# The samples' new scan states: four plain fp32 products of 32 rows in four PSUM banks in place of eight fp32r products of split operands

## The chip, the core and the metric

The kernel runs on one core of one Trainium2 chip. The metric is the device time of one execution in microseconds. Five engines work side by side, each through its own list of instructions in order: TensorE (PE in the profile, with its weight loads as PEld), VectorE (DVE), ScalarE (ACT), GpSimd (POOL) and SyncE (SP). Here SP issues most of the DMAs, and POOL issues the stores of intermediate results besides some small arithmetic. PE writes its products into eight banks of PSUM; DVE and ACT read them from there. A product that is queued on PE waits until its operands are written and its bank has been read out.

## The reference

One inference step of a hybrid encoder layer for two groups of requests that share the weights: a prompt of 1024 tokens, and 8 sample batches of 16 tokens each. Each token goes through one wide input projection, then through band attention and through a Mamba-2 scan, whose results are merged and projected out. The change touches one line of the scan, the new state, and of it the part for the samples alone:

```python
def step(h, inp):
    x, d, bk, ck = inp
    a_cs = jnp.cumsum(d * ag, axis=1)
    ...
    xdt = x * d[..., None]
    ...
    to_end = jnp.exp(a_cs[:, -1:] - a_cs)
    h_new = h * jnp.exp(a_cs[:, -1])[..., None, None] + jnp.einsum('blgn,blgep->bgepn', bk, xdt * to_end[..., None])
    return h_new, y_in + y_st
```

For the samples a chunk is the 16 tokens of a batch, so the scan is one step. For each of the 8 batches and each pair of heads, the product of `bk` (16 tokens by 128 state entries) and the weighted `x` (16 tokens by 128 channels) is added to the decayed old state. There are 32 heads, handled as 16 pairs; four pairs form a group that shares `bk`.

## The kernel before, in words

The 1152 tokens (1024 prompt, then 128 sample tokens) lie along the columns. Every wide projection is made in fp16 with two-part operands: a weight block and a token block are each split into a high and a low part, and three products (high by high, high by low, low by high) are summed in PSUM. These are the products of `dense`, lines 872, 873 and 875, 128x384 each; `dense_tok` (lines 925 to 927) does the same for attention, and `quad_dense` (lines 781 to 783) for the last projections.

The stages are: attention of 8 head units with their projections; then 16 pairs of scan heads, each with its own projections; then the output projections. The pair's small work (`ssd`, lines 1864 to 2095) runs between the products of the projections. For a pair p, `main` does in order:

- It turns `x` to have tokens in the rows, and scales it in two ways: `xd`, and `xw`, which also carries the decay to the end of the chunk. `tokb` holds `bk` of the group with the tokens in the rows. Rows 0 to 127 of the last 128 columns are the 128 sample tokens, 16 rows a batch.
- Prompt states: products of line 1990, sums on DVE (line 1999), stored at line 2004.
- Outputs: products of lines 2018, 2025 and 2038 and their sums on DVE (lines 2031, 2043, 2044, 2051).
- The old sample states `h0` are scaled on DVE (line 2053); the outputs are stored at line 2055, issued by POOL.
- New sample states, lines 2059 to 2074: eight products of line 2063 (128x256, all 128 rows) and two additions to `h0` on DVE (line 2072), then the store of line 2081, issued by POOL.

A product that contracts over 128 rows would mix the batches, so the rows of the other batches have to be zero. Before the change this goes so. For each half of the batches (64 token rows) `bk` is split into a high part and a rest (`hi`, `lo`, lines 1962 to 1965, once a group), and `xw` likewise (lines 1971 and 1972, once a pair), in the type fp32r. The high part of `xw` sits in the half's own 64 rows and the rest in the other 64, so that a product over 128 rows sums both. `masked(q)` then copies this, on POOL, twice over into 256 columns, each copy with the rows of all batches but one zeroed (line 1979). There are two places for such masked operands, so `masked(2)` and `masked(3)` wait until the products of `masked(0)` and `masked(1)` have read theirs. Each masked operand is multiplied by `hi` and by `lo`.

PSUM has three pools: `d` with three banks for the projections, `g` with three banks for small work, and `s` with one place of two banks (`pss`), which the products of line 2018 and attention use.

The order of each engine's instructions is made ahead of the run by the class `Order`: it puts every instruction at a time by a table of costs, takes the earliest in program order that can go, keeps a margin for inputs that come from other engines (1000 ns for PE, 2500 ns for a DMA), and allots the PSUM places. Consecutive products of the same tile shape in parts of the array form one unit.

Of the kernel before, what the change touches and what calls it, by code (L numbers as in the profile page):

```python
# [49 lines left out]
C_ID, C_U, C_UB, C_ONE, C_BLK, C_BM, C_SEL, C_S4, C_BM4 = 0, 128, 256, 384, 512, 640, 648, 680, 712  # L50
NCONST = 716
# [369 lines left out]
def trunk_kernel(ctx: ExitStack, tc: tile.TileContext, h, again):  # L421
# [18 lines left out]
    def pg(cols=512):  # L440
        return psg.tile([P, 512], F32, tag="g", name=nm("g"))[:, :cols]
# [35 lines left out]
    bmask4 = cst[:, C_BM4:C_BM4 + 4]  # L477

# [39 lines left out]
    L_ST = rarena.set_layout(0, [("b", 4, P), ("s", 2, P), ("x", 2, 2 * P)])  # L518
# [1311 lines left out]
    def group_dense(g, lay):  # L1830
        res = grp[g] = {"b": [], "c": [], "sq": None, "st": None}
        yield from conv_gen(16 + g, lay, res["b"])
        yield from conv_gen(20 + g, lay, res["c"])
# [30 lines left out]
    def ssd(p):  # L1864
# [62 lines left out]
        def main():  # L1927
# [27 lines left out]
            if res["st"] is None:  # L1955
                bs = res["st"] = []
                for j in range(2):
                    rw, ro = slice(64 * j, 64 * j + 64), slice(64 - 64 * j, 128 - 64 * j)
                    b_ = tokb.ap[rw, NP:]
                    hi = yield from walloc(L_ST, "b", P)  # L1960
                    lo = yield from walloc(L_ST, "b", P)
                    nc.scalar.activation(hi.r[rw], b_, AF.Copy)
                    nc.scalar.activation(hi.r[ro], b_, AF.Copy)
                    nc.vector.tensor_tensor(lo.r[rw], b_, hi.ap[rw], ALU.subtract)
                    nc.vector.tensor_tensor(lo.r[ro], b_, hi.ap[rw], ALU.subtract)
                    bs.append((hi, lo))
            xs = []
            for j in range(2):
                rw, ro = slice(64 * j, 64 * j + 64), slice(64 - 64 * j, 128 - 64 * j)
                t = yield from walloc(L_ST, "s", P)  # L1970
                nc.scalar.activation(t.r[rw], xw.ap[rw, NP:], AF.Copy)
                nc.vector.tensor_tensor(t.r[ro], xw.ap[rw, NP:], t.ap[rw], ALU.subtract)
                xs.append(t)

            def masked(q):

                t = alloc(L_ST, "x", 2 * P)
                i = 2 * (q % 2)
                nc.gpsimd.tensor_tensor(t.r.rearrange("p (b n) -> p b n", n=P), xs[q // 2].ap.unsqueeze(1).to_broadcast([P, 2, P]),
                                        bmask4[:, i:i + 2].unsqueeze(2).to_broadcast([P, 2, P]), ALU.mult)  # L1980
                return t

            xm = [masked(0), masked(1)]
# [75 lines left out]
            pss_ = [pg(), pg()]  # L2059
            for q in range(4):  # L2060
                j, i = q // 2, q % 2
                for w, b_ in enumerate(res["st"][j]):
                    nc.tensor.matmul(pss_[j][:, 2 * i * P:2 * (i + 1) * P], b_.r, xm[q].r, start=w == 0, stop=w == 1)
                xm[q].free()
                if q < 2:
                    xm.append(masked(q + 2))
                yield 215
                if q == 1:
                    yield from pause(4500)
                if i:  # L2070
                    c = slice(4 * j * P, (4 * j + 4) * P)
                    nc.vector.tensor_tensor(h0.ap[:, c], h0.ap[:, c], pss_[j], ALU.add)
            for t in xs + [xw]:
                t.free()
# [8 lines left out]
            if p % PPG == PPG - 1:  # L2083
                s = res["sq"]
                for t in (tokb, res["cbm"], res["ct"], *res["st"][0], *res["st"][1]):
                    t.free()
# [2140 lines left out]
```

## Time and profile before

| what | value |
|---|---|
| median of 3 runs | 1749.53 us (1746.5 to 1753.16) |
| profiled execution: its time | 1750.06 us |
| profiled execution: its span | 1748.3 us |
| granted TensorE clock, mean | 0.995 |
| products of line 2063 | 128, from 703.0 to 1359.0 us |
| bytes moved by DMA | 284.92 MB |

The span is the time from the first to the last instruction of the profiled execution; 1.8 us lie around it. The columns of the profile's lists of groups are: line, engine, operation, what it writes and reads, shapes and count, then busy time in us, mean ns of one, idle time of the engine just before them and what ended it. A PE shape such as 128*32 is the part of the array that a product occupies, rows by columns. A product of plain fp32 stands in the trace as two records, one of fp16 or fp32r as one. The duration of a PE record contains its way through the array, so records overlap; what a product costs is read from the distance between starts.

### The profile page before, as it was taken

The page shows a single profiled execution, that of the slowest core. Times are in us where ns is not written, and L with a number is a line of the kernel's source. Part 1 is how long each engine was busy: PE and PEld are TensorE (multiplying, and loading weights), DVE is VectorE, ACT ScalarE, POOL GpSimd, SP SyncE. Part 2 cuts the span into 40 slices and gives each one's busy share as a digit, 9 for nine tenths or more (in the row PEclk, how much of TensorE's full clock was granted, in tenths as well). Part 3 has the DMA queues.
Part 4 walks back from the last instruction along what each step waited for, and adds up shares of the span by engine and source line. Part 5 has one row for each costly group of instructions (what it writes and reads, how often), then busy time and mean ns, then how long its engine had stood idle before and what let it go on. Part 6 is the DMA issues. An engine that isn't in the chain of part 4 may idle for free.

```text
span 1748.3 us, 35611 instructions
## 1 busy us (share of the span) xinstructions
PE 1718.8 (98%) x14013; PEld 1113.4 (64%) x14013; DVE 1312.6 (75%) x2477; ACT 995.8 (57%) x1987; POOL 351.4 (20%) x624
## 2 busy tenths in 40 slices
PE   7999999999999999999999999999999999999998
PEld 3556556556556566667666766676666677666676
DVE  6458667877776967787878777777778787897694
ACT  8766555566465665655755556555666633455340
POOL 0233233224134011232312122212112200000000
PEclk9999999999999999999999999999999999999999
DMA  9248888988878584643554355434555655421141
GB/s 383 76 126 204 191 218 204 200 221 196 203 226 173 148 214 133 171 131 118 170 160 116 118 133 175 140 117 108 155 165 194 244 192 222 146 89 54 58 157 72
DMA packets 267433, 284.92 MB, mean 163 GB/s; under 512 B 199724, under 2 KB 200376, under 8 KB 267256
## 3 DMA queue, kind: packets, MB, share of 16 engines
q1 hardware_dynamic: 258296, 253.90, 52.4%
q0 software_dynamic: 8960, 28.65, 4.4%
q8 instruction: 112, 1.84, 0.4%
q14 instruction: 65, 0.53, 0.1%
HBM read 192.70 MB, written 43.66 MB: 135 GB/s over the span
## 4 chain that ended last, share of the span: by engine, by line
PE 87%; ACT 4%; DVE 4%; DMA 2%; issue 1%; POOL 1%; SPq 0%; DVEq 0%; ACTq 0%; POOLq 0%
PE d L872 16%; PE d L873 16%; PE d L875 16%; PE d L925 5%; PE d L927 5%; PE d L926 5%; PE g L1531 2%; PE s L2018 2%; PE g L1990 2%; PE g L2038 1%; PE s L783 1%; PE s L781 1%; PE s L782 1%; PE s L1578 1%; PE g L1578 1%
## 5 line engine op out<-in xcount | busy, mean ns | idle before, releaser
L872 PE MATMUL d<-arena 128*128 128x384 f16 x1872 | 611.8, 327 | 1.4 <-ACT arena L1706 1.4
L873 PE MATMUL d<-arena 128*128 128x384 f16 x1872 | 610.7, 326 | 0.0
L875 PE MATMUL d<-arena 128*128 128x384 f16 x1872 | 610.7, 326 | 0.0
L875 PEld LDWEIGHTS <-arena 128*128 128x128 f16 x1896 | 185.7, 98 | 122.9 <-issue 0.5
L872 PEld LDWEIGHTS <-arena 128*128 128x128 f16 x1896 | 185.7, 98 | 121.5 <-issue 8.6
L873 PEld LDWEIGHTS <-arena 128*128 128x128 f16 x1896 | 185.7, 98 | 113.5 <-issue 2.0
L628 ACT ACTIVATE arena<-arena 128x1024 bf16<-128x1024 f32 (+4 forms) x185 | 184.6, 998 | 106.1 <-DMA arena<-in_wall_dram 65.4
L925 PE MATMUL d<-arena 128*128 128x384 f16 (+1 forms) x568 | 186.8, 329 | 0.0
L637 DVE SCALAR_TENSOR_TENSOR arena<-arena 128x1024 f16<-128x1024 f32 (+2 forms) x133 | 160.0, 1209 | 35.1 <-ACT arena L636 33.3
L927 PE MATMUL d<-arena 128*128 128x384 f16 (+1 forms) x568 | 186.1, 328 | 0.0
L926 PE MATMUL d<-arena 128*128 128x384 f16 (+1 forms) x568 | 186.1, 328 | 0.0
L636 ACT ACTIVATE arena<-arena 128x1024 f16<-128x1024 f32 (+2 forms) x133 | 135.5, 1021 | 85.3 <-PE d L873 15.5
L1471 ACT ACTIVATE arena<-arena 128x640 f32<-128x640 f32 (+4 forms) x144 | 100.8, 701 | 62.9 <-DVE arena L1474 62.4
L1729 DVE SCALAR_TENSOR_TENSOR arena<-arena 128x1176 f32<-128x1176 f32 x72 | 107.3, 1490 | 2.3 <-issue 0.9
L1917 ACT ACTIVATE arena<-arena 128x128 f32<-128x128 f32 x288 | 89.9, 390 | 25.9 <-DMA arena<-acs_d 25.7
L925 PEld LDWEIGHTS <-arena 128*128 128x128 f16 x576 | 56.3, 98 | 50.8 <-issue 17.5
L1507 DVE SCALAR_TENSOR_TENSOR arena<-arena 128x640 f16<-128x640 f32 (+4 forms) x128 | 87.0, 713 | 0.0
L1366 ACT ACTIVATE arena<-d 128x256 f32<-128x256 f32 x71 | 26.8, 377 | 96.1 <-PE d L927 96.0
L927 PEld LDWEIGHTS <-arena 128*128 128x128 f16 x576 | 56.4, 98 | 38.4 <-issue 0.2
L1399 POOL TENSOR_SCALAR arena<-arena 128x16 f32<-128x16 f32 (+1 forms) x24 | 9.4, 392 | 353.5 <-DVE arena L1372 353.4
L926 PEld LDWEIGHTS <-arena 128*128 128x128 f16 x576 | 56.4, 98 | 32.8
L1474 DVE CUSTOM_DVE_ANT_0 arena<-s,arena 128x320 f32<-128x320 f32 (+4 forms) x128 | 60.3, 503 | 19.4 <-PE s L1578 9.5
(271 smaller groups left out, 3150.0 us busy)
## 6 DMA issues: line engine op xcount, KB each, us to landing
arena<-in_wall_dram SPq DMA_DIRECT2D x85, 512.0 KB
arena<-acs_d SPq DMA_DIRECT2D x32, 576.0 KB
arena<-in_kc_dram SPq DMA_DIRECT2D x64, 256.0 KB
arena<-in_vc_dram SPq DMA_DIRECT2D x64, 256.0 KB
arena<-in_wada_dram SPq DMA_DIRECT2D x24, 512.0 KB
arena<-in_xT_dram SPq DMA_DIRECT2D x16, 576.0 KB
gate_d<-arena POOLq DMA_DIRECT2D x48, 192.0 KB, 3.6
arena<-eacs_d SPq DMA_DIRECT2D x32, 288.0 KB
```

The lines of the kernel that those rows point to most:

```text
L628: keep(nc.scalar.activation(junk[:, :n], x, AF.Square, scale=scale * n ** -0.5, accum_out=sums[:, c:c + 1]))
L636: keep(nc.scalar.activation(hi, x, AF.Copy, scale=scale))
L637: keep(nc.vector.scalar_tensor_tensor(lo, x, scale, hi, ALU.mult, ALU.subtract))
L872: nc.tensor.matmul(ps, hi.r[:, wc], kh.r[:, tok], start=k == 0, stop=False)
L873: nc.tensor.matmul(ps, hi.r[:, wc], kl.r[:, tok], start=False, stop=False)
L875: nc.tensor.matmul(ps, lo.r[:, wc], kh.r[:, tok], start=False, stop=k == nk - 1)
L925: nc.tensor.matmul(ps, kh.r[:, tok], wh, start=k == 0, stop=False)
L926: nc.tensor.matmul(ps, kh.r[:, tok], wl, start=False, stop=False)
L927: nc.tensor.matmul(ps, kl.r[:, tok], wh, start=False, stop=k == KT - 1)
L1471: nc.scalar.activation(p, p, AF.Exp, bias=sm_[:, 4 + e:5 + e], scale=-1.0, accum_out=sm_[:, 6 + e:7 + e])
L1729: nc.vector.scalar_tensor_tensor(yc, r.ap[:, j:j + n], w4[:, i, j:j + 1], yc, ALU.mult, ALU.add)
L1917: nc.scalar.activation(me[e].ap[:, cs], me[e].ap[:, cs], AF.Relu, scale=-1.0, bias=a4[:, c, hds[e]:hds[e] + 1])
```

## The change

The split parts go (the pools `b` and `s` of the fp32r store, and the instructions that made them). `xw` is masked once a pair, by POOL, with a new mask of two columns: column 0 is one where the batch of a row is even, column 1 where it is odd. A product over 32 rows (two batches) with this 256-column operand then gives the states of both batches side by side. Four such products, one for each 32 rows, in plain fp32, go to four banks: two of the pool `g` and both of the pool `s`. The pause of 4500 in the middle goes. DVE adds the four results in three additions: one for each `g` bank (256 columns), and one for both `s` banks.

```diff
-C_ID, C_U, C_UB, C_ONE, C_BLK, C_BM, C_SEL, C_S4, C_BM4 = 0, 128, 256, 384, 512, 640, 648, 680, 712
-NCONST = 716
+C_ID, C_U, C_UB, C_ONE, C_BLK, C_BM, C_SEL, C_S4, C_BM4, C_BM2 = 0, 128, 256, 384, 512, 640, 648, 680, 712, 716
+NCONST = 718
...
+    bmask2 = cst[:, C_BM2:C_BM2 + 2]
...
-    L_ST = rarena.set_layout(0, [("b", 4, P), ("s", 2, P), ("x", 2, 2 * P)])
+    L_ST = rarena.set_layout(0, [("x", 2, 2 * P)])
...
-            if res["st"] is None:
-                bs = res["st"] = []
-                for j in range(2):
-                    rw, ro = slice(64 * j, 64 * j + 64), slice(64 - 64 * j, 128 - 64 * j)
-                    b_ = tokb.ap[rw, NP:]
-                    hi = yield from walloc(L_ST, "b", P)
-                    lo = yield from walloc(L_ST, "b", P)
-                    nc.scalar.activation(hi.r[rw], b_, AF.Copy)
-                    nc.scalar.activation(hi.r[ro], b_, AF.Copy)
-                    nc.vector.tensor_tensor(lo.r[rw], b_, hi.ap[rw], ALU.subtract)
-                    nc.vector.tensor_tensor(lo.r[ro], b_, hi.ap[rw], ALU.subtract)
-                    bs.append((hi, lo))
-            xs = []
-            for j in range(2):
-                rw, ro = slice(64 * j, 64 * j + 64), slice(64 - 64 * j, 128 - 64 * j)
-                t = yield from walloc(L_ST, "s", P)
-                nc.scalar.activation(t.r[rw], xw.ap[rw, NP:], AF.Copy)
-                nc.vector.tensor_tensor(t.r[ro], xw.ap[rw, NP:], t.ap[rw], ALU.subtract)
-                xs.append(t)
-            def masked(q):
-                t = alloc(L_ST, "x", 2 * P)
-                i = 2 * (q % 2)
-                nc.gpsimd.tensor_tensor(t.r.rearrange("p (b n) -> p b n", n=P), xs[q // 2].ap.unsqueeze(1).to_broadcast([P, 2, P]),
-                                        bmask4[:, i:i + 2].unsqueeze(2).to_broadcast([P, 2, P]), ALU.mult)
-                return t
-            xm = [masked(0), masked(1)]
+            xm = yield from walloc(L_ST, "x", 2 * P)
+            nc.gpsimd.tensor_tensor(xm.ap.rearrange("p (i n) -> p i n", n=P), xw.ap[:, NP:].unsqueeze(1).to_broadcast([P, 2, P]),
+                                    bmask2.unsqueeze(2).to_broadcast([P, 2, P]), ALU.mult)
...
-            pss_ = [pg(), pg()]
-            for q in range(4):
-                j, i = q // 2, q % 2
-                for w, b_ in enumerate(res["st"][j]):
-                    nc.tensor.matmul(pss_[j][:, 2 * i * P:2 * (i + 1) * P], b_.r, xm[q].r, start=w == 0, stop=w == 1)
-                xm[q].free()
-                if q < 2:
-                    xm.append(masked(q + 2))
-                yield 215
-                if q == 1:
-                    yield from pause(4500)
-                if i:
-                    c = slice(4 * j * P, (4 * j + 4) * P)
-                    nc.vector.tensor_tensor(h0.ap[:, c], h0.ap[:, c], pss_[j], ALU.add)
-            for t in xs + [xw]:
-                t.free()
+            sp = pss.tile([P, 2, 512], F32, tag="s", name=nm("s"))
+            pss_ = [pg(2 * P), pg(2 * P), sp[:, 0, :2 * P], sp[:, 1, :2 * P]]
+            for j in range(4):
+                rw = slice(32 * j, 32 * j + 32)
+                nc.tensor.matmul(pss_[j], tokb.ap[rw, NP:], xm.ap[rw], start=True, stop=True, tile_position=(32 * j, 0))
+            xm.free()
+            xw.free()
+            yield 500
+            for j in range(0, 4, 2):
+                c = slice(4 * j // 2 * P, (4 * j // 2 + 4) * P)
+                c4 = h0.ap[:, c].rearrange("p (b n) -> p b n", b=2)
+                if j:
+                    nc.vector.tensor_tensor(c4, c4, sp[:, :, :2 * P], ALU.add)
+                else:
+                    for i in range(2):
+                        nc.vector.tensor_tensor(c4[:, i], c4[:, i], pss_[i], ALU.add)
...
+    const[:, C_BM2:C_BM2 + 2] = (i[:, None] // NS) % 2 == np.arange(2)[None, :]
```

The lines of the changed kernel lie 1 to 25 below or above those of the old one; the products of line 2063 are now in line 2038, the additions of line 2072 in lines 2046 and 2049, the mask of line 1979 in line 1957, and the store of line 2055 in line 2030.

Because `Order` plans the whole program anew, instructions move beyond the lines of the diff. Three places matter for the prediction.

On PE, at the first pair, where the products of the states stand between those of a projection. Before (each row is line, operation, written and read tile, shape of the moving operand, count; a second group of four follows 57 rows later):

```order
L875 LDWEIGHTS arena
L875 MATMUL d_8830<-arena 128x384
L2063 MATMUL g_8847<-rarena 128x256 x4
L872 LDWEIGHTS arena
L872 MATMUL d_8830<-arena 128x384
```

Now:

```order
L876 LDWEIGHTS arena
L876 MATMUL d_8817<-arena 128x384
L2038 MATMUL g_8835<-rarena,arena 128x256
L2038 MATMUL g_8836<-rarena,arena 128x256
L2038 MATMUL s_8834<-rarena,arena 128x256 x2
L873 LDWEIGHTS arena
L873 MATMUL d_8817<-arena 128x384
```

The two groups of four products have become one group at the place of the first, with tiles of `g` and `s`.

On POOL, around the store of the second pair's outputs (`y_d`). Before:

```order
L2004 DMA out_hp_dram<-arena 128x128
L2055 DMA y_d<-arena 128x1152
L1979 TENSOR_TENSOR rarena<-rarena,arena 128x256
L1717 COPY arena<-arena 128x3
L1718 COPY arena<-arena 128x24
L1979 TENSOR_TENSOR rarena<-rarena,arena 128x256
L1719 DMA out_conv_dram<-arena 128x27
L2081 DMA out_hs_dram<-arena 128x1024
```

Now:

```order
L1957 TENSOR_TENSOR rarena<-arena 128x256
L1979 DMA out_hp_dram<-arena 128x128
L2030 DMA y_d<-arena 128x1152
L1718 COPY arena<-arena 128x3
L1719 COPY arena<-arena 128x24
L1720 DMA out_conv_dram<-arena 128x27
L2056 DMA out_hs_dram<-arena 128x1024
```

Before, two masks stand behind the store of `y_d`, the second also behind two copies of the convolution's tail; now the pair's only mask stands ahead of its stores.

On ACT, at the start of the last stage, around the copy of the modulation's product out of PSUM (line 2283 before, 2258 now, in `mod_gate`). Before (line 2141 makes the high part of a scan output, and line 628 measures levels):

```order
L820 ACTIVATE arena<-d_15357 128x288
L2141 ACTIVATE arena<-arena 128x1152
L628 ACTIVATE arena<-arena 128x1152
L628 ACTIVATE arena<-arena 128x1024
L2283 ACTIVATE arena<-g_15517 128x512
L636 ACTIVATE arena<-arena 128x1024 x2
```

Now:

```order
L821 ACTIVATE arena<-d_15175 128x288
L637 ACTIVATE arena<-arena 128x1024 x2
L2258 ACTIVATE arena<-g_15367 128x512
L637 ACTIVATE arena<-arena 128x512
L817 ACTIVATE arena<-s_15445 128x288 x2
L637 ACTIVATE arena<-arena 128x1024
L2258 ACTIVATE arena<-g_15504 128x512
L2116 ACTIVATE arena<-arena 128x1152
```

The copy of line 2283 stood behind the high part of line 2141; now both copies of line 2258 stand ahead of that step (line 2116).

More of the change, by code (lines that the diff above doesn't have):

```diff
@@ L1830, in group_dense @@
     def group_dense(g, lay):
-        res = grp[g] = {"b": [], "c": [], "sq": None, "st": None}
+        res = grp[g] = {"b": [], "c": [], "sq": None}
         yield from conv_gen(16 + g, lay, res["b"])
@@ L2084, in main @@
                 s = res["sq"]
-                for t in (tokb, res["cbm"], res["ct"], *res["st"][0], *res["st"][1]):
+                for t in (tokb, res["cbm"], res["ct"]):
                     t.free()
```

## The prediction

> **What bounds the kernel now.** The page comes first: the busy times, then the shares of the chain that ended last; then the busy time of each engine in the stretch of the scan pairs.
>
> ```profile
> PE 1718.8 (98%) x14013; PEld 1113.4 (64%) x14013; DVE 1312.6 (75%) x2477; ACT 995.8 (57%) x1987; POOL 351.4 (20%) x624
> ...
> PE 87%; ACT 4%; DVE 4%; DMA 2%; issue 1%; POOL 1%; SPq 0%; DVEq 0%; ACTq 0%; POOLq 0%
> ```
>
> ```profile
> 655.00:1350.00 695.00, 692.40 (x5250) 468.20 (x5248) 531.07 (x795) 416.23 (x793) 161.03 (x278) 1.00 0.48 143
> ```
>
> PE is busy for 98% of the span and carries 87% of the chain. Where the pairs are worked (655 to 1350 us), it is busy for 692.40 of 695.00 us at the full clock, while DVE has 531 us of work, ACT 416 and POOL 161. So a us of PE work saved there is a us saved, and a us of PE waiting too; work saved on the other three counts only where PE waits for it. Next I read the timeline of PE around the products of line 2063 (columns: start in us, duration, engine, line, what, count, and in brackets the wait and who ended it):
>
> ```profile
> 702.83 0.33 PE L873 MATMUL d<-arena 128*128 128x384 f16 x1
> 702.99 0.33 PE L875 MATMUL d<-arena 128*128 128x384 f16 x1
> 703.02 0.77 PE L2063 MATMUL g<-rarena 128*128 128x256 f32 x4
> 703.63 0.34 PE L872 MATMUL d<-arena 128*128 128x384 f16 x1
> ```
>
> A product of a projection follows the one before by 0.16 us. With four products of line 2063 between, the distance is 0.64 us, so these four cost 0.48 us, a pair's eight 0.96 us and 16 pairs 15.4 us. PE stood still for one of these groups:
>
> ```profile
> 743.08 0.33 PE L875 MATMUL d<-arena 128*128 128x384 f16 x1
> 743.51 0.50 PE L2063 MATMUL g<-rarena 128*128 128x256 f32 x2
> 746.51 0.80 PE L2063 MATMUL g<-rarena 128*128 128x256 f32 x2 [2.50 <-POOL rarena L1979]
> 747.11 0.54 PE L872 MATMUL d<-arena 128*128 128x384 f16 x1
> 747.44 0.53 PE L873 MATMUL d<-arena 128*128 128x384 f16 x1
> ...
> 749.59 0.33 PE L875 MATMUL d<-arena 128*128 128x384 f16 x1
> ```
>
> ```profile
> 747.00:749.00 2.00, 2.00 (x8) 0.94 (x8) 2.00 (x3) 2.00 (x8) 2.00 (x3) 0.50 0.98 273
> ```
>
> It waited for a mask of POOL. Afterwards the products follow each other by 0.33 us, at a granted clock of 0.50, up to 749.59. Why the mask was late, POOL's timeline tells:
>
> ```profile
> 742.28 0.54 POOL L2055 DMA_DIRECT2D y_d<-arena  x1 [12.95 <-DVE arena L2051]
> 742.83 0.62 POOL L1979 TENSOR_TENSOR rarena<-rarena,arena 128x256 fp32r<-128x256 f32 x1
> 743.51 1.21 POOL L1717 COPY arena<-arena 128x3 f32<-128x3 f32 x1
> 744.67 1.22 POOL L1718 COPY arena<-arena 128x24 f32<-128x24 f32 x1
> 745.85 0.61 POOL L1979 TENSOR_TENSOR rarena<-rarena,arena 128x256 fp32r<-128x256 f32 x1
> ```
>
> The masks of the second half stood behind a store that waited 12.95 us for DVE, and the last also behind two copies.
>
> **The products themselves.** Removed: 0.96 us of PE a pair. Added: four products of 256 columns in plain fp32, each on 32 rows of the array. No row of this trace has that form, so I bound it. Plain fp32 alone:
>
> ```profile
> 720.70 1.05 PE L1990 MATMUL g<-arena 128*128 128x128 f32 x8
> 721.59 0.33 PE L872 MATMUL d<-arena 128*128 128x384 f16 x1
> ```
>
> Eight records are four products of 128 columns, in 0.89 us: 0.22 us each, and 0.44 us for 256 columns. Four of those one after another make 1.78 us; four at once 0.44 us. Products in parts of the array do run at once here:
>
> ```profile
> 118.59 0.33 PE L927 MATMUL d<-arena 128*128 128x384 f16 x1
> 118.84 1.06 PE L1633 MATMUL s<-arena 128*32 128x512 f32 x8
> 119.72 0.40 PE L1636 MATMUL s<-arena 128*32 128x128 f32 x8
> 120.06 0.34 PE L925 MATMUL d<-arena 128*128 128x384 f16 x1
> ...
> 200.40 0.33 PE L927 MATMUL d<-arena 128*128 128x384 f16 x1
> 200.66 0.58 PE L1578 MATMUL s<-arena 64*128 64x320 f16 x6
> 201.17 0.34 PE L925 MATMUL d<-arena 128*128 128x384 f16 x1
> ```
>
> Lines 1633 and 1636 are fp32 in four parts of 32 columns: four products of 512 and four of 128 columns. They cost 120.06 - 118.59 - 0.16 = 1.31 us. One lane of 640 columns would take 5 x 0.22 = 1.11 us, all in a row 4.44 us. So all four parts run at once, and 0.20 us go to changing the shape, there and back. Line 1578 is fp16 in two parts of 64 rows: six products of 320 columns cost 0.77 - 0.16 = 0.61 us. At 0.16 us for 384 columns, three steps are 0.41 us and six 0.81; again both parts run at once, plus 0.20 us. The new form joins the type of the one with the row parts of the other, so I take four at once: 0.44 + 0.20 = 0.64 us a pair, 0.32 us less than before, 16 x 0.32 = **5.1 us saved**. The ends are 0.64 us and 1.98 us (all in a row, with the change of shape), that is 5.1 us saved or 16.3 us lost.
>
> By the Trainium skill, "TensorE: Matmul & The Clock Gate", Part 3 (measured speedup), four row parts of 32 with 512 columns ran 3.07 times as fast as in a row, not 4 times. By that the group would be an estimated 1.78 / 3.07 + 0.20 = 0.78 us and the saving 2.9 us; the row of line 1633 speaks for the full four, in column parts.
>
> **The stall behind POOL.** From the end of the product at 743.08 (743.24) to the next projection's product at 747.11 lie 3.87 us, of which 0.48 us are the group: 3.39 us lost. Then eight products took 749.59 - 747.11 = 2.48 us in place of 8 x 0.16 = 1.28: 1.20 us more. Together 4.6 us. In the changed order a pair has one mask, and it stands ahead of the pair's stores, so that no product waits for a mask behind them. What would be late next is POOL's own stores, for which PE does not wait. I take **4.6 us saved**; the other end is 0, if another stall takes its place.
>
> **A second stall, moved by the new order.** At the start of the last stage PE waits for ACT, which has waited for DVE:
>
> ```profile
> 1394.08 1.16 ACT L2141 ACTIVATE arena<-arena 128x1152 f16<-128x1152 f32 x1 [6.10 <-DVE arena L2231]
> ...
> 1397.61 0.58 ACT L2283 ACTIVATE arena<-g 128x512 f32<-128x512 f32 x1
> ```
>
> ```profile
> 1395.44 0.29 PE L783 MATMUL g<-arena 128*128 128x288 f16 x1
> 1398.24 1.88 PE L1010 MATMUL g<-arena 128*128 128x9 f32 x8 [2.52 <-ACT arena L2283]
> ...
> 1404.90 0.29 PE L781 MATMUL d<-arena 128*128 128x288 f16 x1
> ```
>
> ```profile
> 1399.00:1404.00 5.00, 5.00 (x23) 3.49 (x23) 4.22 (x11) 1.79 (x2) 0.00 (x0) 0.50 0.86 277
> ```
>
> 288 columns take 0.12 us at 0.16 for 384, so PE loses 1398.24 - 1395.56 = 2.68 us, and then half of the 6.66 us up to 1404.90 at the half clock, 3.3 us: 6.0 us. In the changed order the copy of line 2283 stands ahead of line 2141 on ACT, so what made it wait no longer does. But the DMA and the DVE step that were late stay late, and on DVE the additions of the next products stand behind them still. Between none and 6.0 us I take the half, **3.0 us saved**, since the wait may only move.
>
> **What lies beside.** These groups shrink or go (columns: busy us, mean ns, idle before):
>
> ```profile
> L2063 PE MATMUL g<-rarena 128*128 128x256 f32 x128 | 25.9, 320 | 2.6 <-POOL rarena L1979 2.5
> ...
> L1979 POOL TENSOR_TENSOR rarena<-rarena,arena 128x256 fp32r<-128x256 f32 x64 | 52.7, 838 | 49.3 <-PE g L2063 44.3 <-DVE rarena L1972 4.7
> ...
> L2072 DVE TENSOR_TENSOR arena<-arena,g 128x512 f32<-128x512 f32 x32 | 21.8, 681 | 8.4 <-PE g L2063 8.4
> ...
> L1971 ACT ACTIVATE rarena<-arena 64x128 fp32r<-64x128 f32 x32 | 9.8, 306 | 20.4 <-DVE arena L1949 18.9 <-POOL rarena L1979 1.1
> L1972 DVE TENSOR_TENSOR rarena<-arena,rarena 64x128 fp32r<-64x128 f32 x32 | 9.5, 298 | 4.2 <-ACT rarena L1971 3.4
> ```
>
> POOL loses 48 of 64 masks, 48 x 0.838 = 40 us. ACT loses 32 copies, 9.8 us, and DVE 32 differences, 9.5 us, besides those once a group. DVE's additions become three a pair; two of 256 columns cost between one and two of 681 ns, so at most 16 x 0.68 = 11 us more. PE's 692 of 695 us cover all of this, and I cost it at nothing; without that cover DVE would at worst be 1.4 us longer. The group now needs two places of `g` and the place `s` at once, and behind it on PE stand projection products, which would wait with it. All idle time of PE in this stretch is the 2.6 us before line 2063 (692.40 of 695.00), so its waits for PSUM are covered by the plan so far, and I cost the new one at nothing; the upper end is the third rival.
>
> **Sum.** 5.1 + 4.6 + 3.0 = 12.7 us off the span of 1748.3 us is 1735.6 us. The profiled execution took 1750.06 us, 0.5 us over the median of 1749.53, so against the median it is 1736.8: I say **1737 us**.
>
> **Rivals.**
> Slower: *the four row parts run in a row.* Plain fp32 in row parts is the one form the trace lacks, and it reads a full width of 128 columns of weights in each part, where lines 1633 and 1636 read 32. The group is 1.98 us, PE loses 16.3 us and regains 7.6 by the stalls: 1758 us. It decides from a group of 0.96 + 7.6 / 16 = 1.44 us on. Against it stand lines 1633 and 1578.
>
> *Two at a time.* Each fp32 product is two records. If the second record of one part has to start before the first of the next part, two records run at once at most: five steps of 0.22 us + 0.20 = 1.30 us, 16 x 0.34 = 5.4 us lost, 7.6 regained: 1747 us. Line 1633's two records a product against it, all four parts at once. The Trainium skill, same page, Part 3 (what overlaps), has products start and end strictly in program order; by that, if the records are in program order product by product, this rival would hold.
>
> *The stalls stay.* The products cost what I say, but the last stage's wait remains, and a wait for the place `s`, for two places of `g` or for a late DVE takes the place of POOL's, with the half clock behind it as both stalls of the profile have: 5.1 us saved alone, 1744 us. For it speaks that the plan of the whole program is new; against it that the 2.6 us before line 2063 are PE's only idle time in the pairs' stretch, and that POOL, which caused it, is out of the way.
>
> **How the numbers follow.** Forecast 0.48; the stalls stay 0.20; two at a time 0.10; in a row 0.15; other mishaps on the slow side 0.07. A measurement of this kernel tells no less than 0.5% (8.7 us, to 1740.8 or 1758.3) from no change. Forecast: 0.41 of its 0.48 below 1740.8, the rest between; the stalls stay: 0.02 below, 0.18 between; two at a time: 0.10 between; in a row: its 1758 us lie at the bound, and a longer group is one more thing to be late, so 0.10 above and 0.05 between; mishaps: 0.07 slower. So faster 0.43, same 0.40, slower 0.17. The range: below, all 6.0 us of the second stall gained, and some 3 us of scatter as between the runs shown: 1731. Above, it takes in the stalls that stay and two at a time, with one more stall of 6 us: 1754. The forecast's own range is 1733 to 1743.
>
> **What would show it.** In the changed profile, where four products of line 2038 stand between two projection products, these start 0.80 us apart (0.64 + 0.16); 1.46 would be two at a time, 2.14 in a row. PE has no wait for line 1957, and the granted clock shows no 0.50 between 655 and 1350 us. On ACT, line 2258 does not follow a wait for DVE. A wait of PE for lines 2046 or 2006 would be the place `s`. The prediction is wrong if the group is over 0.96 us, or if PE's waits between 655 and 1410 us add up to more than the 6 us that they are now.

## The result, and the profile after

The changed kernel takes 1738.56 us, the median of 6 runs (1737.88 to 1740.68), and the kernel before, on the same chip, 1748.76 us (6 runs, 1746.0 to 1753.16). The ratio is 0.9943, with a 95% interval of 0.9932 to 0.9955: 10.2 us less, where 12.7 us less had been forecast. The profiled execution took 1739.89 us, with a span of 1738.1 us, 10.2 us below the span before.

First the page's busy times and its chain, then the busy time of each engine in the pairs' stretch, as shown of before (columns: stretch, its length, busy time and count of instructions of PE, PEld, DVE, ACT and POOL, granted clock, DMA share, GB/s):

```profile
PE 1712.6 (99%) x14013; PEld 1099.1 (63%) x14013; DVE 1290.9 (74%) x2445; ACT 978.8 (56%) x1939; POOL 311.3 (18%) x576
...
PE 91%; ACT 4%; DVE 3%; issue 1%; DMA 1%; POOL 0%; SPq 0%; DVEq 0%; ACTq 0%; POOLq 0%
```

```profile
655.00:1350.00 695.00, 693.76 (x5277) 459.15 (x5276) 511.63 (x765) 400.66 (x751) 121.71 (x235) 1.00 0.49 146
```

PE is still what bounds the kernel. POOL's 161 us in the stretch have become 122, ACT's 416 have become 401 and DVE's 531 have become 512; none of that was on the path. PE's timeline around the first pair's products:

```profile
702.72 0.33 PE L876 MATMUL d<-arena 128*128 128x384 f16 x1
702.97 0.48 PE L2038 MATMUL g<-rarena,arena 32*128 32x256 f32 x2
702.98 0.48 PE L2038 MATMUL s<-rarena,arena 32*128 32x256 f32 x2
703.29 0.38 PE L2038 MATMUL g<-rarena,arena 32*128 32x256 f32 x2
703.30 0.38 PE L2038 MATMUL s<-rarena,arena 32*128 32x256 f32 x2
703.62 0.34 PE L873 MATMUL d<-arena 128*128 128x384 f16 x1
```

The first records of all four products start within 0.02 us, the second records 0.32 us later, the next projection 0.33 us after those. From projection to projection it is 703.62 - 702.72 = 0.90 us, so the group costs 0.90 - 0.16 = 0.74 us. In 15 of the 16 pairs it is the same to 0.01 us. In the fourth pair PE waits in the middle of the group, and the projections behind it run at the half clock:

```profile
822.79 0.69 PE L2038 MATMUL g<-rarena,arena 32*128 32x256 f32 x2
824.72 0.48 PE L2038 MATMUL g<-rarena,arena 32*128 32x256 f32 x1 [1.24 <-ACT arena L1850]
...
825.43 0.50 PE L873 MATMUL d<-arena 128*128 128x384 f16 x1
825.72 0.53 PE L874 MATMUL d<-arena 128*128 128x384 f16 x1
```

```profile
825.00:829.00 4.00, 4.00 (x20) 2.19 (x18) 2.70 (x7) 3.62 (x6) 0.85 (x3) 0.57 0.42 147
```

The second product of `g` has no place until ACT has read out a transposed block (line 1850, in `group_lat`). The mean clock of these 4 us is 0.57, so another 4 x 0.43 = 1.7 us go after the wait. This stall is new. POOL's timeline in the second pair, where the old kernel stood still:

```profile
722.96 0.61 POOL L1957 TENSOR_TENSOR rarena<-arena 128x256 f32<-128x256 f32 x1 [0.74 <-DVE arena L1950]
...
737.77 0.54 POOL L2030 DMA_DIRECT2D y_d<-arena  x1 [11.40 <-DVE arena L2026]
740.86 1.10 POOL L1718 COPY arena<-arena 128x3 f32<-128x3 f32 x1 [2.56 <-ACT arena L1710]
741.91 0.20 POOL L1719 COPY arena<-arena 128x24 f32<-128x24 f32 x1
742.40 0.55 POOL L1720 DMA_DIRECT2D out_conv_dram<-arena  x1 [0.29 <-POOL arena L1719]
```

The store waits nearly as long as before (11.40 us, 12.95 then) and the copies behind it for another 2.56 us, but no mask stands behind them: this pair's only mask was made at 722.96. In the last stage (ACT, then PE):

```profile
1389.54 0.60 ACT L2258 ACTIVATE arena<-g 128x512 f32<-128x512 f32 x1 [2.66 <-PE g L1005]
```

```profile
1391.50 0.29 PE L784 MATMUL d<-arena 128*128 128x288 f16 x1
1391.62 0.96 PE L1011 MATMUL g<-arena 128*128 128x9 f32 x8
```

The copy of the modulation waits for PE alone, and PE's products of line 1011 follow at once. The second stall is gone whole. The account in the profiled executions:

| term | forecast | profile |
|---|---|---|
| products, 16 x (0.96 - 0.74) | -5.1 | -3.5 |
| stall behind POOL at 743 us | -4.6 | -4.6 |
| stall at the start of the last stage | -3.0 | -6.0 |
| new wait for a place of `g`, 1.2 + half clock 1.7 | 0 | +2.9 |
| PE's wait at 1430.70 us for ACT (line 817) | 0 | +0.8 |
| sum | -12.7 | -10.4; the span: -10.2 |

Shifts of some 0.3 us elsewhere are left out.

### The profile page after: what moved, and what is told of

Its sections match the earlier page's. It is cut to its first block, busy times and chain, and to the rows that moved or that the text cites. A ratio compares the mean times of both kernels' runs of the same rounds, so it can differ in the third digit from the quotient of the medians.

```text
span 1738.1 us, 35467 instructions
## 1 busy us (share of the span) xinstructions
PE 1712.6 (99%) x14013; PEld 1099.1 (63%) x14013; DVE 1290.9 (74%) x2445; ACT 978.8 (56%) x1939; POOL 311.3 (18%) x576
## 4 chain that ended last, share of the span: by engine, by line
PE 91%; ACT 4%; DVE 3%; issue 1%; DMA 1%; POOL 0%; SPq 0%; DVEq 0%; ACTq 0%; POOLq 0%
PE d L873 17%; PE d L876 17%; PE d L874 17%; PE d L926 5%; PE d L928 5%; PE d L927 5%; PE g L1532 2%; PE s L1993 2%; PE g L1965 2%; PE g L2013 1%; PE s L782 1%; PE s L784 1%; PE s L783 1%; PE s L1579 1%; PE g L1579 1%; PE g L1667 1%
## 5 line engine op out<-in xcount | busy, mean ns | idle before, releaser
L1730 DVE SCALAR_TENSOR_TENSOR arena<-arena 128x1176 f32<-128x1176 f32 x72 | 103.8, 1441 | 3.0 <-issue 1.3
```

Source lines behind the costliest of these rows:

```text
L1730: nc.vector.scalar_tensor_tensor(yc, r.ap[:, j:j + n], w4[:, i, j:j + 1], yc, ALU.mult, ALU.add)
```

## The experiments

Each compares with the kernel before, run beside it on one chip.

**What a group of products costs.** Extra products ahead of the group, another kind in each pair:

```diff
+            extra = {1: [(0, 32, 256)], 2: [(0, 32, 256), (1, 32, 256)], 3: [(j, 32, 256) for j in range(3)],
+                     4: [(j, 32, 256) for j in range(4)], 5: [(j, 32, 256) for j in range(4)] * 2,
...
+            for j, rows, cols in extra:
+                rw = slice(rows * j, rows * j + rows)
...
+                nc.tensor.matmul(full[j][:, :cols], tokb.ap[rw, NP:], mv, start=True, stop=True, **kw)
             for j in range(4):
```

> The changed kernel with extra products ahead of the group of line 2051 in pairs 1 to 13, another kind in each pair, whose results the group then overwrites; the output is that of the changed kernel and the time of the whole is not read. Read is the distance between the projection products on both sides, less that of pair 0 without extras. The group measured 0.74 us, two passes 0.32 us apart plus 0.10, where the prediction had two passes of 0.22 plus 0.20. Theory A, a fixed 0.10 us a pass on top of the columns (weights loaded anew for each half of an fp32 product): four more parts of 256 columns add 0.64 us, of 128 columns 0.42, of 64 columns 0.32, of 512 columns 1.08, and one part alone costs as much as four. Theory B, four parts at once share something and stream at 0.69 of the speed: 256 columns 0.64, 128 columns 0.32, 64 columns 0.16, 512 columns 1.28, and one or two parts cost 0.44. Theory C, it is all change of shape: four more parts of 256 columns add only 0.44. Two parts of 64 rows: A 0.64, B 0.44. Each part twice in a row (0,0,1,1,2,2,3,3): 1.28 by A and B if a part's second product can run beside the next part's first, four times 0.32 or more if it cannot. Products of the full 128 rows and 256 columns: 0.44 us each, and a change of shape more.

PE's timeline in pair 4, where the group stands twice:

```profile
874.47 0.33 PE L876 MATMUL d<-arena 128*128 128x384 f16 x1
874.72 0.48 PE L2048 MATMUL g<-rarena,arena 32*128 32x256 f32 x2
...
875.04 0.38 PE L2048 MATMUL g<-rarena,arena 32*128 32x256 f32 x2
...
875.26 0.38 PE L2051 MATMUL g<-rarena,arena 32*128 32x256 f32 x2
...
875.48 0.38 PE L2051 MATMUL g<-rarena,arena 32*128 32x256 f32 x2
...
875.80 0.34 PE L873 MATMUL d<-arena 128*128 128x384 f16 x1
```

The steps are 0.32 us from the first records to the second, and then 0.22 and 0.22. The distance is 1.33 us where a single group (pair 0) has 0.90, so four more products cost 0.43 us. The other kinds, in the same way:

| extra | adds, us |
|---|---|
| four parts of 256 columns; the same twice | 0.43; 0.86 |
| four parts of 512, 128, 64 columns | 0.86; 0.22; 0.22 |
| one part alone; two parts | 0.41; 0.42 |
| each part twice in a row (eight products) | 0.88 |
| two parts of 64 rows, alone between projections | 0.73 |
| one product of all 128 rows, alone between projections | 0.43 |
| two products of all 128 rows | 0.86 |
| two parts of 64 rows, the same twice | 1.07 |

(In pair 3 a wait fell into the group, and three parts were not measured.) Theory C holds: four parts together cost what one product of the full array costs, 0.43 us, and a fixed 0.74 - 0.43 = 0.31 us is paid for going to the parts and back, once for a group of any size. A and B, which put it into each pass, are out (0.64 expected). Two parts of 64 rows pay 0.30 us too, and a group of 32-row parts right behind four products of 64 rows pays again: 1.07 - 2 x 0.43 = 0.21 us. "Two at a time" is out with its reason: products issued in the order 0, 0, 1, 1 cost no more than in the order 0, 1, 2, 3. The rows of pair 1, with one more product in part 0 (line 2048) ahead of the group, show how parts start:

```profile
741.21 0.48 PE L2048 MATMUL g<-rarena,arena 32*128 32x256 f32 x1
741.23 0.48 PE L2051 MATMUL g<-rarena,arena 32*128 32x256 f32 x1
741.23 0.48 PE L2051 MATMUL s<-rarena,arena 32*128 32x256 f32 x2
...
741.75 0.59 PE L2051 MATMUL g<-rarena,arena 32*128 32x256 f32 x2
```

The last row, two records of one product, is taken for the group's own product in part 0, the part that the extra one held (the records give the tile, not the part). It is issued ahead of the other three and starts 0.52 us after them.

**The group twice in every pair.**

```diff
             for j in range(4):
                 rw = slice(32 * j, 32 * j + 32)
                 nc.tensor.matmul(pss_[j], tokb.ap[rw, NP:], xm.ap[rw], start=True, stop=True, tile_position=(32 * j, 0))
+            for j in range(4):
+                rw = slice(32 * j, 32 * j + 32)
+                nc.tensor.matmul(pss_[j], tokb.ap[rw, NP:], xm.ap[rw], start=True, stop=True, tile_position=(32 * j, 0))
```

> The changed kernel, with the group of four products issued twice in all 16 pairs (the second overwrites the first with the same numbers). Theory: PE bounds the pairs, and a group behind a group costs two passes of 0.32 us, 16 x 0.64 = 10.2 us more than the changed kernel: a ratio to the kernel before of 1.000 where the changed kernel has 0.9943. If the group were mostly change of shape: 16 x 0.44 = 7.0 us, 0.998. If PE's time in the pairs were hidden behind something else: 0.9943. The first wait for a place of g at 823 us may move.

Measured: 1745.61 us, a ratio of 0.9990 (0.9979 to 1.0000), 7.0 us over the changed kernel's 1738.56. That kernel was timed on another chip; by the ratios, each to the kernel before beside it, it is 0.0047 x 1748 = 8.2 us, and the two intervals together leave some 3 us either way. From the rows above, 16 x 0.43 = 6.9 us, and in this run's profile the distance across the doubled group is 1.33 us in 15 of 16 pairs. So the rows choose the branch with 7.0 us over the theory's 10.2, which the time alone would not exclude. Within that margin a us of PE work in the pairs is a us of time.

**The store of `y_d` off POOL's queue.** In the kernel before (`store` is POOL's, `dma` SP's):

```diff
-            store(y_d[p], x.ap)
+            dma(y_d[p], x.ap)
```

> The kernel before, with one edit: the store of line 2055 is issued by SP in place of POOL, so that no mask of line 1979 stands behind its wait for DVE. The orders of PE, DVE and ACT are the same as before. Theory (the term of 4.6 us for the stall behind POOL): PE's wait at 743.5 to 746.5 us and the half clock after it go, and the time falls by 4.6 us, a ratio of 0.9974. Rivals: SP, whose queue holds the weight loads, now waits for DVE in POOL's place and PE gets a new wait for weights, so that half of the 4.6 us or more comes back; or the masks were late for another reason, and the time stays (1.000).

Measured: 1757.64 us, 1.0052 (1.0037 to 1.0068), 10 us slower than the 1747.59 beside it. The stall stayed. POOL, then ACT, then PE:

```profile
743.17 1.10 POOL L1717 COPY arena<-arena 128x3 f32<-128x3 f32 x1 [2.75 <-ACT arena L1709]
744.22 0.20 POOL L1718 COPY arena<-arena 128x24 f32<-128x24 f32 x1
744.38 1.59 POOL L1979 TENSOR_TENSOR rarena<-rarena,arena 128x256 fp32r<-128x256 f32 x1
```

```profile
741.67 1.16 ACT L2056 ACTIVATE arena<-arena 128x1152 f32<-128x1152 f32 x1 [2.73 <-DVE arena L2051]
742.75 0.36 ACT L1709 ACTIVATE arena<-d 128x256 f32<-128x256 f32 x1
```

```profile
746.02 0.80 PE L2063 MATMUL g<-rarena 128*128 128x256 f32 x2 [3.20 <-POOL rarena L1979]
```

With the store away the mask stands behind the copies alone, these wait for ACT, and ACT's next step ahead is held by the same DVE step that held the store (line 2051). So the store was one of two ways from that step to the mask, and taking one away gains nothing. The time is longer for another reason: PE's last product starts 2.8 us later than before (1743.0 against 1740.2), part of it a new wait of 1.56 us for DVE at 1106 us, and the end after it takes longer (columns: stretch, its length, busy PE, PEld, DVE, ACT, POOL):

```profile
1743.00:1759.70 16.70, 0.17 (x3) 0.06 (x2) 2.05 (x6) 0.00 (x0) 0.00 (x0) 0.59 0.10 33
```

16.7 us, where before 8.0 us lay between the last product's start and the end (1740.24 to 1748.27), with no more work in it. In the records POOL's closing DRAIN instruction lasts 8.56 us, before 1.21.

**The modulation's copy ahead on ACT.** In the kernel before, in `mod_gate`:

```diff
-            yield from pause(6000)
+            yield from pause(0)
             ps, p2 = pg(), pg(36)
```

> The kernel before, with one edit in mod_gate: the pause of 6000 ahead of the modulation's products is 0, so that the first copy of line 2283 stands ahead of line 2141 on ACT, as it does in the changed kernel; the states' products stay as before. Theory (the second stall): the wait of 2.68 us and the half clock after it go whole, 6.0 us, a ratio of 0.9966. Rival (the half that the prediction took): the DMA and the DVE step that were late stay late and PE waits for them at another place, 3.0 us or less gained (0.9983 or nearer to 1). The stall behind POOL at 743 us stays in both.

Measured: 1758.56 us, 1.0060 (1.0047 to 1.0073): 11 us slower. PE:

```profile
1394.41 1.92 PE L1004 MATMUL g<-arena 128*32 128x512 f32 x4 [5.05 <-DMA arena<-in_wada_dram]
1397.03 1.88 PE L1010 MATMUL g<-arena 128*128 128x9 f32 x8 [0.69 <-ACT arena L2283]
```

The edit moved the products with the copy, ahead of the load of their weights: the wait for ACT fell from 2.52 to 0.69 us, and one of 5.05 us for the DMA came, with a half clock of 10.2 us in place of 6.8. That is 3.2 + 1.7 = 4.9 us; new waits of 0.7 to 0.9 us each for DVE (two) and ACT (two) add some 3 us, and the rest stays open. Both theories missed this; what the stall is worth it does not tell.

**Both edits together.**

> The kernel before, with both edits: the store of line 2055 issued by SP and the modulation's pause at 0. The products of the states are the old ones, 128 of them in fp32r with split operands. Theory: both stalls go, 4.6 + 6.0 = 10.6 us, a ratio of 0.9939, so that the old products are as fast as the changed kernel (0.9943), whose own 3.5 us of shorter products its new wait at 823 us takes back. Rival: the changed kernel's gain hangs on its products or its one mask, and the stalls turn up elsewhere: 0.997 or more.

Measured: 1767.46 us, 1.0110 (1.0093 to 1.0126): the losses of the two add up (10 + 11 us, 20 measured), and it says no more than they do.

**The pause alone.** In the kernel before, one part of the change:

```diff
                 yield 215
-                if q == 1:
-                    yield from pause(4500)
```

> The kernel before, with one part of the change alone: the pause of 4500 between the two halves of the states' products goes. Products, split operands and four masks a pair stay. The plan shifts in the whole program, and in the last stage both copies of line 2283 now stand ahead of line 2141's step on ACT, as in the changed kernel. Theory: the second stall goes with the old products too, 6.0 us, a ratio of 0.9966, while masks three and four still stand in POOL's queue and PE goes on waiting for one of them (0.9966 or somewhat more). Rival 1: the four masks in a row, 0.84 us each, make PE wait in many pairs, 16 x 1 us or more, a ratio of 1.006 or more. Rival 2: the second stall comes from elsewhere and stays: 1.000.

Measured: 1743.87 us, 0.9982 (0.9972 to 0.9992), 4.1 us less. In the last stage the wait of line 1010 is gone, though DVE still waits for `yb` (DVE), and a smaller wait for ACT has come 15 us earlier (PE):

```profile
1394.54 1.42 DVE L2229 SCALAR_TENSOR_TENSOR arena<-arena 128x1152 f32<-128x1152 f32 x1 [2.39 <-DMA arena<-yb]
```

```profile
744.61 0.50 PE L2063 MATMUL g<-rarena 128*128 128x256 f32 x2 [1.22 <-POOL rarena L1979]
...
1376.86 0.28 PE L781 MATMUL d<-arena 128*128 128x288 f16 x1 [1.79 <-ACT arena L1821]
```

Neither wait brings a half clock. So the old products keep a wait for the mask (1.22 us in place of 2.50), and the stall of the last stage goes with the order on ACT, as the theory had it, against a new wait of 1.79 us. By these rows some 7 us should be gone: 6.0 of the last stage and, behind POOL, 4.6 less the 1.5 still lost there, against the 1.79. Measured are 4.1, so some 3 us are lost in places not accounted for here. Rival 1 is out.

**Two masks off POOL.** In the kernel before:

```diff
-                nc.gpsimd.tensor_tensor(t.r.rearrange("p (b n) -> p b n", n=P), xs[q // 2].ap.unsqueeze(1).to_broadcast([P, 2, P]),
+                (nc.gpsimd if q < 2 else nc.vector).tensor_tensor(t.r.rearrange("p (b n) -> p b n", n=P), xs[q // 2].ap.unsqueeze(1).to_broadcast([P, 2, P]),
```

> The kernel before, with one edit: the third and fourth mask of each pair (line 1979) are made by DVE in place of POOL, so that they stand behind neither POOL's store nor its copies. PE's order is nearly the same. On DVE they stand, in the second pair, behind the scaling of line 2051 for which the store of line 2055 waited, and behind the next two steps. Theory (the place in POOL's queue makes the wait at 743 us): the 2.5 us and the half clock behind them go, 4.6 us less, a ratio of 0.9974; 32 masks more on DVE, 0.4 us each, hide behind PE. Rival: DVE itself is the late one there, the masks come behind line 2051 and one or two steps of 0.7 to 1.4 us, PE waits nearly as long, and the time stays at 0.999 to 1.000. The second stall in the last stage stays in both.

Measured: 1742.53 us, 0.9966 (0.9953 to 0.9979), 5.4 us less. The busy times of the pairs' stretch, then DVE, POOL and PE at the old stall:

```profile
655.00:1350.00 695.00, 695.00 (x5278) 470.36 (x5277) 537.40 (x828) 421.04 (x799) 137.70 (x252) 1.00 0.48 144
```

```profile
738.09 1.36 DVE L2051 SCALAR_TENSOR_TENSOR arena<-arena 128x1152 f32<-128x1152 f32 x1
...
741.15 1.36 DVE L2078 TENSOR_TENSOR arena<-arena 128x1152 f32<-128x1152 f32 x1
742.43 0.76 DVE L1979 TENSOR_TENSOR rarena<-rarena,arena 128x256 fp32r<-128x256 f32 x2
```

```profile
739.74 0.54 POOL L2055 DMA_DIRECT2D y_d<-arena  x1 [11.52 <-DVE arena L2051]
...
742.50 0.41 POOL L1718 COPY arena<-arena 128x24 f32<-128x24 f32 x1
```

```profile
744.11 0.77 PE L2063 MATMUL g<-rarena 128*128 128x256 f32 x4
```

Both masks are ready at 743.2 us, PE's four products run at 744.11, and PE has no wait left between 655 and 1410 us. But the plan shifted too. In the kernel before DVE does the step of line 2051 behind one of line 1923 that waits for ACT:

```profile
739.36 1.36 DVE L1923 TENSOR_TENSOR arena<-arena 128x1152 f32<-128x1152 f32 x1 [1.26 <-ACT arena L1921]
740.63 1.35 DVE L2051 SCALAR_TENSOR_TENSOR arena<-arena 128x1152 f32<-128x1152 f32 x1
```

Here it does it ahead of that step, 2.5 us earlier, and POOL is through with the copies at 742.91. A mask of 0.61 us behind them would be made at an estimated 743.5 us, still before PE asks for it. So the run shows that the old products can do without the stall; how much of this the masks' place on DVE does, and how much the earlier step, it does not part. The stall of the last stage went as well:

```profile
1387.79 1.42 DVE L2231 SCALAR_TENSOR_TENSOR arena<-arena 128x1152 f32<-128x1152 f32 x1 [0.16 <-DMA arena<-yb]
```

```profile
1391.60 0.58 ACT L2283 ACTIVATE arena<-g 128x512 f32<-128x512 f32 x1
```

The copy of line 2283 still stands behind line 2141 on ACT, but DVE waits only 0.16 us for `yb` (3.35 before), and PE goes on without a wait. So this is the old kernel with its old products and without its two stalls. It lies 4.0 us above the changed kernel by the medians (1742.53 - 1738.56), and 0.0023 x 1748 = 4.0 by the ratios, with some 3 us either way by the two intervals: that agrees with the products' own worth, 3.5 us from their rows, and does not measure it more closely.

**The new wait for a place of `g`.** In the changed kernel, the copies of `group_lat` on DVE (in a second form, only the second of the three):

```diff
-            nc.scalar.activation(tok.ap[:, c], pt[:, :n * P], AF.Copy)
+            nc.vector.tensor_copy(tok.ap[:, c], pt[:, :n * P])
```

> The changed kernel, with one edit: the copies of group_lat out of PSUM (line 1850) are made by DVE in place of ACT. Theory: the wait of 1.4 us inside the group of products at 823 us is for a place of g which ACT reads out late, behind two long steps; DVE is idle there, so the wait goes, and the half clock of 3.4 us behind it, 1.4 + 1.7 = 3.1 us less than the changed kernel: a ratio to the kernel before of 0.9925 where the changed kernel has 0.9943. Rival: another place is late in its turn (DVE has 74% of the span to do, and takes 12 more steps), and the time stays at 0.9943 or more.

Measured: 1738.37 us, 0.9949 (0.9937 to 0.9961). The wait in the group is gone and no half clock is left in the pairs, but two waits of 0.31 and 0.62 us for DVE have come. In time nothing is gained. To tell why, the changed kernel, this one and the second form ran side by side.

> The changed kernel itself once more, beside the next two on one chip. Theory: 1738.6 us, a ratio of 0.9943, with the wait for a place of g inside the group of products at 823 us again, and a half clock behind it in this profile or not: in the profiles so far a wait of 1.24 us brought it in one run and one of 0.95 us did not in another, so whether it comes is left to where the wait falls. Rival: the half clock of 3.4 us follows this wait in every run.

> The changed kernel with the copies of group_lat on DVE, once more, beside the changed kernel on the same chip. Theory: the wait of 1.4 us goes, 0.9 us of other waits come (0.31 and 0.62 us for DVE, as in its first profile), and the half clock that the wait brings in some runs goes: 0.5 to 2.2 us less than the changed kernel. Rival: no difference that is measured, 0.3 us or less either way.

> The changed kernel, where of the three copies of group_lat a group only the second, the one that was read out late, is on DVE. Theory: the wait at 823 us goes and DVE, with 4 steps more in place of 12, brings no new wait: 1.4 us or more less than the changed kernel, a ratio of 0.9935 or less. Rival: the plan of the whole program shifts again (its PE order differs in half of the pairs), and a wait of the same size turns up in another place: 0.9943 or more.

Measured: 1738.57 us (0.9946, 0.9929 to 0.9963), 1738.41 (0.9942, 0.9926 to 0.9959) and 1738.86 (0.9948, 0.9931 to 0.9965). No difference. The PE row of the wait in each, in this order:

```profile
824.81 0.48 PE L2038 MATMUL g<-rarena,arena 32*128 32x256 f32 x1 [0.80 <-ACT arena L1850]
```

```profile
825.12 0.33 PE L1849 MATMUL g<-arena 128*128 128x128 f32 x1 [0.39 <-DVE arena L1857]
827.04 0.49 PE L1855 MATMUL g<-arena 128*128 128x128 f32 x2 [0.62 <-DVE arena L2049]
```

```profile
826.04 0.33 PE L1849 MATMUL g<-arena 128*128 128x128 f32 x1 [1.24 <-DVE arena L1860]
```

In this execution of the changed kernel the wait is 0.80 us with no half clock behind it, and the span is 1736.3 us, 1.8 less than in the first profile. So the 2.9 us of the first profile are one execution's, and every cure brings back about 1 us of waits for DVE. The changed kernel is as fast as any version that was timed.

## Why the prediction was right, step by step

The forecast of 1737 us (its own range 1733 to 1743) is met with 1738.56. Of its terms one held to the digit; the others were off by +1.6, -3.0, +2.9 and +0.8 us, and that they come to only 2.3 us is luck.

- **The products.** The mechanism held: all four parts run at once, at 0.43 us where 0.44 was worked out from line 1990. The projections on both sides start 0.90 us apart, where 0.80 had been named as the sign. Mis-sized was the term of 0.20 us for changing the shape and back: it is 0.31 us, 0.10 us of it between a group's first and second records. The rows of lines 1633 and 1578, from which the 0.20 came, each had half of the new form (fp32, row parts); the sum of the two was not in the trace. That is 16 x 0.10 = 1.6 us less saved, 3.5 us in place of 5.1. The estimate by the Trainium skill ("TensorE: Matmul & The Clock Gate", Part 3, measured speedup), 0.78 us, lies nearer to the 0.74, but the trace puts the loss elsewhere: four parts take the 0.43 us of one full product, a factor of 4, and the rest is the change of shape. With that counted in, the rows here give an estimated 4 x 0.86 / (0.86 + 0.31) = 2.9 for four parts of 512 columns, the form of the Trainium skill's 3.07.
- **In a row, two at a time.** Both are out by the group of 0.74 us. The rule of the Trainium skill, same page, Part 3 (what overlaps), that products start in program order is not what these records show: in the price list's pair 1 the parts 1 to 3 start within 0.03 us of the extra part 0, and the group's own part 0, issued before them, 0.52 us after them.
- **The stall behind POOL.** It went, and 4.6 us with it: one mask, ahead of the stores. The forecast's account of why it was late was incomplete. It named the store's wait of 12.95 us and the copies as what stood ahead; the run with the store on SP showed that either is enough, since both hang on DVE's step of line 2051. Nor did it name DVE's own order: that step stood behind one that waited for ACT, and in the changed kernel, as in the runs without the pause and with two masks on DVE, it stands ahead and comes earlier. Without the pause it comes early and the masks stay on POOL, and 1.22 us of the wait stay too. So the place in POOL's queue and the late step both count; their shares stay open.
- **The stall of the last stage.** The term "I take the half, since the wait may only move" was mis-sized: it went whole, 6.0 us. The half was a choice between two ends, not worked out from a row. The late step did stay late (DVE waits 1.06 us for `yb` in the changed kernel, 2.39 us without the pause), but with the copy ahead of it on ACT nothing that PE needs stands behind it. That DVE's additions would pass the wait on did not come true. The runs without the pause and with two masks on DVE lose this stall as well, the first by the order on ACT, the second by an earlier load of `yb`; so it hung on where the plan happened to put things, not on the new products.
- **The new wait for two places of `g`.** The forecast cost it at nothing and kept it as a rival. It came, in one pair of 16: 1.24 us and 1.7 us of half clock in the first profile, against the sign that no granted clock of 0.50 shows in the pairs, and 0.80 us without a half clock in the second. Its argument, that PE's waits for PSUM were covered by the plan so far, did not carry over to a group that needs three places at once, in a pair where `group_lat` competes for them.
- **What lay beside.** POOL's 40 us of masks, and the steps saved on ACT and DVE, moved nothing by themselves, as said: DVE's additions are now 32 x 416 ns and 16 x 681 ns, and PE waits for none of them in the pairs.

By the experiments, of the 10 us some 4 are the products' (3.5 by their rows, 4.0 by the times with 3 us either way) and the rest are two stalls, which the old kernel loses by an edit of one engine's name (5.4 us).

## What to carry to other kernels

Price an array shape by a pair of rows, one with the group once and one with it twice: the difference is the work, the rest is the change of shape, and only the second can be saved by putting groups together. A stall seen behind one queue entry may have a second way to the same late step; look who else waits for that step before taking one entry away. And in a kernel planned as a whole, a change's gain can be mostly that of a plan without two accidents, so run the old kernel without them before the credit is given.

## What the runs showed of the hardware

- Plain fp32 in 32-row parts: a group costs 0.43 us for each set of four products of 256 columns plus 0.31 us. 64 columns cost as much as 128 (0.22 us for four parts), so in these rows a set of four products does not get shorter than that.
- The half clock. Its starts in one profile, by the trace's records of the granted clock, lie whole multiples of 3.413 us apart (before: 746.07, 1398.01 and 1742.76 us, 191 and 101 of them). Waits of 2.50, 2.52, 3.20 and 5.05 us brought it, waits of 1.22, 1.56 and 1.79 us did not; 1.24 us brought it in the changed kernel's first profile, where the wait stood between products in parts, and did not in the last run of the copies on DVE. What decides below 2 us stays open. By the Trainium skill ("TensorE: Matmul & The Clock Gate", Part 1) the window is a free-running one of 3413 ns, with which the multiples agree; a whole window of idle, which the Trainium skill names there as the condition, was not needed here: in the 3.413 us before 746.07 PE works until 744.01.
- With 16 stores fewer on POOL's queue, the kernel's end after the last product took 16.7 us in place of 8.0, and 16.1 us in the run with both edits. POOL's closing DRAIN lasts 8.56 us there in both; why stays open.
- A mask of 128x256 on POOL took 0.62 us in the median and 1.83 us at its longest (the kernel before), on DVE 0.41 to 0.43 us (two masks off POOL).
